# A macaron block on one core: the mixer's projections put ahead of its latents, and attention steps put among the last latents

## The chip, the cores and the metric

The kernel runs on one core of a Trainium2 chip. The metric is the device time of one execution in microseconds (us). The core has five engines that take instructions in their own order and wait for each other on semaphores: PE (matrix multiplication, TensorE), DVE (VectorE), ACT (ScalarE), POOL (GpSimd) and SP, which here only issues transfers.

## The reference

One layer on a sequence of 1024 rows of width 1024, in float32:

```
x = x + 0.5 * swiglu(rmsnorm(x), w1_gate, w1_up, w1_down)     # FFN 1, hidden 2816
h = rmsnorm(x) @ w_in    # columns: u 512 | v 512 | c_q 256 | c_kv 128 | k_rope 32
y_a = gelu(u) * (w_s (masked 128x128, per group) @ rmsnorm(gelu(v)) + b)
q  = rmsnorm(c_q)  @ w_uq      # 8 heads of 96 (64 plain + 32 rotary)
kv = rmsnorm(c_kv) @ w_ukv     # 8 heads of 64 (k) + 64 (v); k gets k_rope behind it
q, k = head rmsnorm, then rotation of the last 32 columns
y_b = softmax(q k^T * 96**-0.5, causal in chunks of 64) @ v
x = x + concat(rmsnorm(y_a), rmsnorm(y_b)) @ w_out
x = x + 0.5 * swiglu(rmsnorm(x), w2_gate, w2_up, w2_down)     # FFN 2
x = rmsnorm(x)
```

## The kernel before

Every float32 matrix product is done as three matmuls on operands split into a high and a low part (h and l in the names): hi*hi, hi*lo and lo*hi. Both FFNs use seven products where a plain 2x2 blocking needs eight (P1 to P7, `product`, matmuls at L464); the operands A11, A12, A21, S1 to S4 are quarters of a weight tile and sums of them, xB.. and xT.. the same of the input.

The code is issued step by step. A `Step` is one unit of work, in the order in which the steps are made; `st.before(lead, fn, floor)` puts a preparation (a load, a split) that many steps ahead of it, but not before step `floor`. `run_steps` then issues everything, and a scheduler arranges the instructions of each engine. Tiles of on-chip memory are handed out in a ring, so an instruction that writes a new tile may wait for the last reader of whatever stood there.

The mixer works on eight row tiles of 128 rows. Its steps are named by a letter and a number, and their order is a string in the code:

- u (L844 to L852): 24 matmuls of 512 columns for one row tile, gelu on ACT.
- m and g, for a pair of tiles: m (L859 to L861) is 12 matmuls of 256 columns; g multiplies by gelu(u) on DVE (L868), takes row norms (ACT square L286, POOL power L271) and stores the result to DRAM by two DMAs on POOL's queue (L875).
- a (`latent_in`): 24 matmuls of 416 columns (L722 to L724) for c_q, c_kv and k_rope; ACT copies them out (L770), takes squares (L773) and a square root (L277).
- c (`latent_T`): three transposes on PE (L881), then the split into `chl` by ACT (L290) and DVE (L291).
- k (`key_rope`): rotation of the shared key for two tiles, on POOL.
- l (`latent_tile`): 12 matmuls of 384 columns (L895 to L897) and 6 of 512 (L902 to L904) on `chl`; ACT copies qn (L919), kn (L918), squares (L921, L925) and takes the root r_qk (L277); DVE scales (L933, L934); POOL rotates q and k (L936, then L794, L796, L798).

The attention is a list of items (head, pair of row tiles); the n-th attention step does scores of item n, the transposes of the probabilities of item n-2 and its product with v, and the folding of item n-3. `head_T` (L982 transposes, L986 on ACT) makes the operands of a head. Probabilities are ACT's exp (L1003). Gelu, square root and exp each need another function table on ACT, seen as an instruction ACT_TABLE_LOAD under the line of the function that needs it.

The second FFN's steps are made by `gu2.steps(...)` (L1145): the first two weight tiles' raw quarters are loaded at the steps named by `load_at`, and the transposes of its normalized input (L300) run beside its first products. The first wait of its kind is for x tiles, stored by the first FFN in `x1d`.

Of the kernel before, what the change touches and what calls it, by code (L numbers as in the profile page):

```python
# [20 lines left out]
P = 128  # L21
# [3 lines left out]
NT = S // P  # L25
FH = 2816
NF = FH // P
GW = 512
H = 8
DN, DR, DV = 64, 32, 64  # L30
DQ = DN + DR
QL, KL = 256, 128
LAT = QL + KL + DR
# [27 lines left out]
def f(ap):  # L61
    return ap.bitcast(F32)
# [172 lines left out]
def block(nc, x, positions, ffn1_norm, ffn1_w_gate, ffn1_w_up,  # L235
# [4 lines left out]
    x = x[0]  # L240
    out = out[0]

    def tile_(shape, name, dt=F32):
        return nc.take("sb", shape, name, dt)
# [74 lines left out]
    steps = []  # L319
# [91 lines left out]
    LEAD_LOAD, LEAD_SUM, LEAD_SPLIT = 9, 3, 2  # L411

    class GateUp:
# [80 lines left out]
            t = self.h[u, d] = tile_([P, 512], f"h{d}_{self.tag}{u}")  # L494
            nc.vector.tensor_tensor(t, self.h[u, x0], self.h[u, x1], op=op)

        def steps(self, order, floor=0, loaded=(), load_at=()):
            at = {}
            for u, (pn, ka, kb, pair) in order:
                st = at[u, pn] = Step(lambda u=u, a=(pn, ka, kb, pair): self.product(u, *a))  # L500
                if pn == "P1":
                    for k in range(2):
                        if (u, k) not in loaded:
                            lead = st.index - load_at[u] if u < len(load_at) else LEAD_LOAD - k
                            st.before(lead, lambda u=u, k=k: self.load(u, k))
                if pn == "P6":
                    for which in range(2):
                        st.before(LEAD_SUM - which, lambda u=u, w=which: self.sums(u, w), floor)
                st.before(LEAD_SPLIT, lambda u=u, ka=ka: self.split(u, ka), floor)
            return at  # L510

    EARLY = [(0, BY_NAME["P1"]), (0, BY_NAME["P2"]), (1, BY_NAME["P1"]), (1, BY_NAME["P2"])]
    GU_ORDER = EARLY + [(u, p) for u in range(NU) for p in PRODUCTS if (u, p) not in EARLY]
# [136 lines left out]
    g1 = row_tile(ffn1_norm[0].partition_broadcast(P), "g1")  # L650
# [56 lines left out]
    mx = {"wv": [], "wa": [], "wu": [], "wuq": [], "v": [], "xm": {}, "u": {}, "q": {}, "k": {}, "vv": {}}  # L707
    wiv = w_in[0].rearrange("(k p) c -> p k c", p=P)

    def load_in(key, j, c0, width):  # L710
        mx[key, "raw", j] = load(tile_([P, 4, width], f"raw_{key}{j}"), wiv[:, 4 * j:4 * j + 4, c0:c0 + width])

    def split_in(key, k, width):
        raw = mx[key, "raw", k // 2]
        mx[key].append(q_split(raw[:, 2 * (k % 2):2 * (k % 2) + 2, :], [P, 2, width], f"{key}{k}"))
# [13 lines left out]
    def mix_norm_tile(t):  # L729
        xt = mx.pop(("x", t))  # L730
        xn = tile_([P, D], f"xnm{t}")
        normed(xt, mx["gm"], xn, f"m{t}")
        hv = transposed(xn, f"m{t}")
        xmh = tile_([P, KD, P], f"xmh{t}", F32R)
        xml = tile_([P, KD, P], f"xml{t}", F32R)
        for k in range(2):
            split(hv[k], xmh[:, 4 * k:4 * k + 4, :], xml[:, 4 * k:4 * k + 4, :])
        mx["xm"][t] = (xmh, xml)
# [4 lines left out]
    def v_tile(t):  # L743
        ps = bank(f"vps{t}")
        project(ps, mx["xm"][t], mx["wv"])
        vg = tile_([P, GW], f"vg{t}")
        nc.scalar.activation(vg, ps, AF.Gelu_apprx_tanh)
        sq = tile_([P, GW], f"vsq{t}")
        nc.gpsimd.tensor_tensor(sq, vg, vg, op=ALU.mult)
        ss = small(f"vss{t}", 4)  # L750
        nc.vector.tensor_reduce(ss, sq.rearrange("p (g c) -> p g c", g=4), axis=AX.X, op=ALU.add)
        r = rsqrt_mean(ss, f"v{t}", 4, 128)
        nc.vector.tensor_tensor(sq, vg, mx["gv"], op=ALU.mult)
        v3 = sq.rearrange("p (g c) -> p g c", g=4)
        nc.vector.tensor_tensor(v3, v3, r.unsqueeze(2).to_broadcast([P, 4, P]), op=ALU.mult)
        if t % 2 == 0:
            mx["v"].append([tile_([P, 2, GW], f"v{n}{t}", F32R) for n in "hl"])
        split(sq, mx["v"][-1][0][:, t % 2, :], mx["v"][-1][1][:, t % 2, :])
# [105 lines left out]
    def gmlp_pair(p):  # L864
        u, ps = mx["u"][p], mx.pop(("mix", p))
        for g in range(4):
            gs = slice(g * P, (g + 1) * P)
            nc.vector.scalar_tensor_tensor(u[:, :, gs], ps[:, g], bT[:, g:g + 1], u[:, :, gs],  # L868
                                           op0=ALU.add, op1=ALU.mult)
        for j in range(2):  # L870
            t = 2 * p + j
            ya = tile_([P, GW], f"ya{t}")
            r = row_rstd(u[:, j, :], ya, f"ya{t}", GW)
            nc.vector.scalar_tensor_tensor(ya, u[:, j, :], r, mx["goA"], op0=ALU.mult, op1=ALU.mult)
            nc.gpsimd.dma_start(yAd[rows(t), :], ya)  # L875
# [64 lines left out]
             mx["snq"][:, t:t + 1, :].to_broadcast([P, H, DR]), tab[:, 0], tab[:, 1])  # L940
        mx["q"][t], mx["k"][t], mx["vv"][t] = q_all, k_all, v_t

    vs = [Step(lambda t=t: v_tile(t)) for t in range(NT)]
    sm = {}
    works = {"u": u_tile, "m": mix_pair, "g": gmlp_pair, "a": latent_in, "k": key_rope, "c": latent_T, "l": latent_tile}
    for ch in ("u0 u1 m0 g0 u2 u3 m1 g1 a0 c0 a1 k0 l0 u4 c1 a2 l1 c2 a3 k1 l2 u5 m2 c3 a4 l3 g2 c4 a5 k2 l4 u6 "
               "c5 a6 c6 l5 a7 c7 k3 l6 u7 m3 l7").split():
        sm[ch] = Step(lambda f=works[ch[0]], n=int(ch[1]): f(n))
    v0 = vs[0].index
    vs[0].before(12, mix_gain)  # L950
    for t in range(4):
        steps[v0 - 5 + t].do(lambda t=t: mix_norm_tile(t))
    for t in range(4, NT):
        vs[t].before(4, lambda t=t: mix_norm_tile(t), v0)
    for j in range(2):
        vs[0].before(8 - j, lambda j=j: load_in("wv", j, GW, GW))
        sm["u0"].before(7 - j, lambda j=j: load_in("wu", j, 0, GW))
        sm["a0"].before(9 - j, lambda j=j: load_in("wa", j, 2 * GW, LAT))
    for k, (lv, lu, la) in enumerate(((4, 5, 7), (3, 5, 6), (2, 4, 5), (1, 3, 4))):
        vs[0].before(lv, lambda k=k: split_in("wv", k, GW))  # L960
        sm["u0"].before(lu, lambda k=k: split_in("wu", k, GW))
        sm["a0"].before(la, lambda k=k: split_in("wa", k, LAT))
    vs[0].before(3, v_gain)
    sm["u0"].before(3, spatial_weights)
    sm["u1"].before(0, out_gain)
    sm["a0"].before(6, load_uq)
    sm["a0"].before(4, latent_setup)
    sm["a0"].before(4, load_kv)
    sm["a0"].before(1, split_uq)
    sm["a0"].before(1, split_kv)  # L970
    sm["a0"].before(0, rope_tables)
    sm["l7"].do(lambda: mx.__setitem__("yB", [tile_([P, 4, H, DV], f"yB{i}") for i in range(2)]))

    def head_T(h, half):
        if half == 0:
            mx["qk", h] = [tile_([P, S], f"{n}{h}", F32R) for n in ("qh", "ql", "kh", "kl")]
        tiles = mx["qk", h]
        ps = big(f"T{h}_{half}")
        cs = slice(half * 512, (half + 1) * 512)
        for i, (src, col) in enumerate(((mx["q"], gqcol), (mx["k"], gkcol))):  # L980
            for t in range(4):
                nc.tensor.transpose(ps[:, i * 512 + t * P:i * 512 + (t + 1) * P], src[4 * half + t][:, h, :], ident)  # L982
        for i, col in enumerate((gqcol, gkcol)):
            hi, lo = tiles[2 * i], tiles[2 * i + 1]
            pv = ps[:, i * 512:(i + 1) * 512]
            nc.scalar.activation(hi[:, cs], pv, AF.Copy, scale=col)  # L986
            nc.vector.scalar_tensor_tensor(lo[:, cs], pv, col, f(hi[:, cs]), op0=ALU.mult, op1=ALU.subtract)
# [66 lines left out]
    D1, D2 = 2,3  # L1054
    ORDER = "PSTWF"
    TP = 2,3
    att = {}
    for n in range(len(items) + D2):
        st = att[n] = Step()
        if n == 0:  # L1060
            st.do(lambda: head_T(0, 0))
            st.do(lambda: head_T(1, 0))
        if n == 3:
            st.do(lambda: head_T(0, 1))
            st.do(lambda: head_T(1, 1))
        for op in ORDER:
            if op == "F" and D2 <= n:
                st.do(lambda i=items[n - D2]: folded(*i))
            if op == "P" and D1 <= n < len(items) + D1:
                st.do(lambda i=items[n - D1]: transposed_p(*i))  # L1070
            if n < len(items):
                h, pi = items[n]
                if op == "S":
                    st.do(lambda h=h, pi=pi: score_pair(h, pi))
                if op == "T" and 0 < h < H - 1 and pi in TP:
                    st.do(lambda h=h, pi=pi: head_T(h + 1, pi - TP[0]))
            if op == "W" and D1 <= n < len(items) + D1:
                st.do(lambda i=items[n - D1]: weighted(*i))

    att[0].do(lambda: gmlp_pair(3))  # L1080

    wov = w_out[0].rearrange("(k p) e -> p k e", p=P)
    wo = {}
# [58 lines left out]

    base2 = len(steps)
    gu2 = GateUp("b", xo2, ffn2_w_gate[0], ffn2_w_up[0], hds[1])
    gu2.steps(GU_ORDER, base2, load_at=(base2 - 1, base2))  # L1145
    rest(xo2, base2)

    def normalized(t, x3):
# [59 lines left out]
```

## Time and profile before

| what | value |
| --- | --- |
| time, median of 3 runs | 1774.74 us (1774.66 to 1776.48) |
| profiled execution, its own time | 1775.43 us |
| its span in the trace | 1773.4 us |
| mean granted TensorE clock | 0.989 of full speed |
| PE busy | 1714.4 us, 97% of the span |
| DVE, ACT, POOL busy | 1123.7, 757.0 and 149.5 us |

The span runs from the first to the last instruction on the core; the 2.0 us around it are start and end. The granted clock is given as a share of 2.4 GHz, 0.5 being the other level, 1.2 GHz. A wait in the trace is put down to the engine that came last.

### The profile page before, as it was taken

What the parts mean: (1) busy time and instruction counts of PE and PEld (TensorE: products, weight loads), DVE (VectorE), ACT (ScalarE), POOL (GpSimd) and SP (SyncE); (2) the same over time, 40 slices, a digit from 0 to 9 for tenths busy, and PEclk for the clock granted to TensorE, in tenths of its full rate; (3) what the DMA queues carried; (4) which work ended last, traced back from release to release, by engine and by line L of the source; (5) the groups of instructions that cost most, each with busy time, mean ns of one, the idle gap of its engine ahead of it and who ended that gap; (6) DMA issues with size and microseconds to landing.
All of it is one profiled execution on the core that took longest, in us unless ns stands there. A gap on an engine that the chain in (4) does not pass through costs nothing.

```text
span 1773.4 us, 21088 instructions
## 1 busy us (share of the span) xinstructions
PE 1714.4 (97%) x8132; PEld 1439.8 (81%) x8132; DVE 1123.7 (63%) x1497; ACT 757.0 (43%) x1151; POOL 149.5 (8%) x287
## 2 busy tenths in 40 slices
PE   7999999999999999988799999999999999999998
PEld 5788888888888888877699888778888888888886
DVE  7966556545578666554877644684656655558774
ACT  7523333334334444444777833352333233433442
POOL 2000000000000013322300511100000000000010
PEclk9999999999999999998899999999999999999999
DMA  6323232226844521200000332424233222683531
GB/s 202 115 93 119 98 111 89 96 89 220 311 129 162 183 85 48 69 10 3 13 1 1 120 101 87 140 95 137 76 120 108 95 90 90 231 301 110 179 129 48
DMA packets 122979, 199.48 MB, mean 112 GB/s; under 512 B 11008, under 2 KB 57600, under 8 KB 122880
## 3 DMA queue, kind: packets, MB, share of 16 engines
q1 hardware_dynamic: 118784, 184.52, 30.7%
q0 software_dynamic: 3520, 12.58, 1.8%
q8 instruction: 63, 1.03, 0.2%
q10 hardware_dynamic: 576, 1.05, 0.2%
q14 instruction: 36, 0.29, 0.0%
HBM read 143.07 MB, written 55.05 MB: 112 GB/s over the span
## 4 chain that ended last, share of the span: by engine, by line
PE 89%; DVE 4%; ACT 3%; DMA 1%; POOL 1%; issue 1%; SPq 0%; POOLq 0%; ACTq 0%; DVEq 0%
PE psum L464 45%; PE psum L594 8%; PE psum L596 8%; PE psum L597 8%; PE psum L1026 2%; PE psum L722 2%; PE psum L724 2%; PE psum L723 2%; PE psum L1125 1%; PE psum L1126 1%; PE psum L1128 1%; PE psum L300 1%; PE psum L1036 1%; PE psum L1035 1%; PE psum L997 1%
## 5 line engine op out<-in xcount | busy, mean ns | idle before, releaser
L480 DVE TENSOR_TENSOR P_b<-psum,P_b 128x1024 f32<-128x1024 f32 x33 | 40.3, 1222 | 93.0 <-PE psum L464 93.0
L480 DVE TENSOR_TENSOR P_a<-psum,P_a 128x1024 f32<-128x1024 f32 x33 | 40.3, 1222 | 91.8 <-PE psum L464 91.8
L470 ACT COPY P_b<-psum 128x1024 f32<-128x1024 f32 x33 | 33.4, 1014 | 70.3 <-PE psum L464 68.3
L470 ACT COPY P_a<-psum 128x1024 f32<-128x1024 f32 x33 | 33.4, 1013 | 69.1 <-PE psum L464 69.1
L271 POOL TENSOR_TENSOR r_fin<-ms_fin,mhalf 128x1 f32<-128x1 f32 x8 | 8.0, 1009 | 609.4 <-DVE ms_fin L269 609.3
L291 DVE TENSOR_TENSOR pl<-psum,ph 128x512 fp32r<-128x512 f32 (+1 forms) x80 | 48.5, 630 | 10.8 <-ACT ph L290 10.2
L481 ACT ACTIVATE P_a<-P_a 128x512 f32<-128x512 f32 x33 | 20.8, 631 | 80.8 <-DVE P_a L480 80.7
L1001 DVE TENSOR_REDUCE nm<-psum 128x1 f32<-128x128 f32 (+3 forms) x64 | 46.8, 749 | 11.8 <-PE psum L999 11.5
L481 ACT ACTIVATE P_b<-P_b 128x512 f32<-128x512 f32 x33 | 20.8, 632 | 73.0 <-DVE P_b L480 72.9
L1125 PE MATMUL psum<-woh,yh 128*128 128x512 f32 x128 | 50.5, 396 | 0.0
L1003 ACT ACTIVATE p<-psum,nm 128x128 f32<-128x128 f32 (+3 forms) x64 | 47.7, 750 | 6.4 <-DVE nm L1001 3.4
L1126 PE MATMUL psum<-wol,yh 128*128 128x512 f32 x128 | 50.2, 392 | 0.0
L703 POOL DMA_DIRECT2D x1d<-x_a x8 | 4.6, 580 | 510.6 <-DVE x_a L608 510.5
L1026 PE MATMUL psum<-ident,p 128*128 128x128 f32 x288 | 43.4, 281 | 3.8 <-ACT p L1003 3.8
L1128 PE MATMUL psum<-woh,yl 128*128 128x512 f32 x128 | 44.9, 391 | 0.0
L290 ACT CAST ph<-psum 128x512 fp32r<-128x512 f32 (+1 forms) x80 | 41.7, 559 | 7.0 <-PE psum L1026 6.8
L1036 PE MATMUL psum<-pl,vv 128*128 128x256 f32 x160 | 42.7, 293 | 1.2 <-DVE pl L291 1.2
L1035 PE MATMUL psum<-ph,vv 128*128 128x256 f32 x160 | 43.3, 294 | 0.2 <-ACT ph L290 0.2
L997 PE MATMUL psum<-kh,qh 128*128 128x512 f32 (+2 forms) x96 | 38.6, 404 | 1.0 <-ACT kh L986 0.9
L1026 PEld LDWEIGHTS psum<-ident,p 128*128 128x128 f32 x288 | 34.0, 145 | 6.4 <-ACT p L1003 4.8
L608 DVE SCALAR_TENSOR_TENSOR x_b<-psum,x_b 128x512 f32<-128x512 f32 x32 | 21.0, 686 | 26.9 <-PE psum L597 26.9
L464 PE MATMUL psum<-xB11h_f,A11h_a 128*128 128x512 f32 x88 | 35.4, 405 | 2.6 <-ACT xB11h_f L389 2.6
(525 smaller groups left out, 5753.3 us busy)
## 6 DMA issues: line engine op xcount, KB each, us to landing
raw_a<-in_ffn_w_gate SPq DMA_DIRECT2D x22, 512.0 KB, 4.3
raw_a<-in_ffn_w_up SPq DMA_DIRECT2D x22, 512.0 KB, 5.4
hd<-hS_a SPq DMA_DIRECT2D x44, 256.0 KB, 2.2
raw_b<-in_ffn_w_gate SPq DMA_DIRECT2D x22, 512.0 KB, 4.2
raw_b<-in_ffn_w_up SPq DMA_DIRECT2D x22, 512.0 KB, 5.2
hd<-hS_b SPq DMA_DIRECT2D x44, 256.0 KB, 2.1
aS_a<-hd SPq DMA_DIRECT2D x20, 512.0 KB, 4.2
wB_a<-in_ffn_w_down SPq DMA_DIRECT2D x20, 512.0 KB, 5.6
```

The lines of the kernel that those rows point to most:

```text
L464: mm(o, lhs[:, 4 * m + k, :], rhs[:, k, :], start=pn in FIRST and n == 0, stop=n == 11, skip_group_check=True)
L470: nc.scalar.copy(ev[u, pn], bk)
L480: nc.vector.tensor_tensor(c, bk, c, op=ALU.add)
L594: mm(banks[t], hh[:, j, tl], dh[:, j, :], start=pn in DOWN_FIRST and c == 0 and j == 0, stop=False, skip_group_check=True)
L596: mm(banks[t], hh[:, j, tl], dl[:, j, :], start=False, stop=False, skip_group_check=True)
L597: mm(banks[t], hl[:, j, tl], dh[:, j, :], start=False, stop=c == 5, skip_group_check=True)
L1026: nc.tensor.transpose(ps[:, i * P:(i + 1) * P], prs[j][:, c * P:(c + 1) * P], ident)
L1035: mm(acc[:, 0:256], mx["vv"][c][:, h, :], hi, start=i == 0, stop=False)
L1036: mm(acc[:, 0:256], mx["vv"][c][:, h, :], lo, start=False, stop=i == len(pts) - 1)
L1125: mm(pe[e], yh[:, k, :], wh[:, es], start=k == 0, stop=False)
L1126: mm(pe[e], yh[:, k, :], wl[:, es], start=False, stop=False)
L1128: mm(pe[e], yl[:, k, :], wh[:, e * 512:(e + 1) * 512], start=False, stop=k == KD - 1)
```

## The change

The work stays the same; its order changes in two places.

In the mixer the string of steps puts all u, m and g steps ahead of the first a. The first three attention steps (x0 to x2), which were behind the last latent tile, stand among the last ones; for this their functions move up in the file as they are, with the loop's body as `attend(n)`. The buffer yB is made in the step n == 2.

In the second FFN everything starts one step earlier: the floor of its splits becomes `base2 - 1`, each raw quarter of the first two weight tiles gets its own step for its load, and the split for the third product made is one step ahead of it and not two.

```
-    for ch in ("u0 u1 m0 g0 u2 u3 m1 g1 a0 c0 a1 k0 l0 u4 c1 a2 l1 c2 a3 k1 l2 u5 m2 c3 a4 l3 g2 c4 a5 k2 l4 u6 "
-               "c5 a6 c6 l5 a7 c7 k3 l6 u7 m3 l7").split():
+    for ch in ("u0 u1 m0 g0 u2 u3 m1 g1 u4 u5 m2 g2 u6 u7 m3 g3 a0 c0 a1 k0 l0 c1 a2 l1 c2 a3 k1 l2 c3 a4 l3 c4 a5 k2 l4 "
+               "c5 a6 c6 a7 l5 c7 k3 x0 l6 x1 l7 x2").split():
+        if ch[0] == "x":
+            attend(int(ch[1]))
+            continue
         sm[ch] = Step(lambda f=works[ch[0]], n=int(ch[1]): f(n))
...
-    sm["l7"].do(lambda: mx.__setitem__("yB", [tile_([P, 4, H, DV], f"yB{i}") for i in range(2)]))
...
-    att[0].do(lambda: gmlp_pair(3))
+    for n in range(3, len(items) + D2):
+        attend(n)
...
-                            lead = st.index - load_at[u] if u < len(load_at) else LEAD_LOAD - k
+                            lead = st.index - load_at[u, k] if (u, k) in load_at else LEAD_LOAD - k
...
-                st.before(LEAD_SPLIT, lambda u=u, ka=ka: self.split(u, ka), floor)
+                st.before(LEAD_SPLIT if len(at) != 2 else 1, lambda u=u, ka=ka: self.split(u, ka), floor)
...
-    gu2.steps(GU_ORDER, base2, load_at=(base2 - 1, base2))
+    gu2.steps(GU_ORDER, base2 - 1, load_at={(0, 0): base2 - 2, (0, 1): base2 - 1, (1, 0): base2, (1, 1): base2})
```

What stands on the engines. First ACT, around the second latent tile (qn1, kn1, vv1, sq.. are its copies and squares, r_qk its root, chl2 the split for the third). Before:

```order
L919 COPY qn1_6689<-psum_70 128x8x96 [waits PE_49]
L294 ACTIVATE vv1_6697<-psum_70,rl_6301 128x8x64 [waits DVE_49,PE_49]
L925 ACTIVATE sq1_0_6706<-qn1_6689 128x384 [waits Activation_49]
L918 COPY kn1_6692<-psum_70 128x8x64 [waits DVE_49]
L921 ACTIVATE sk1_6703<-kn1_6692 128x512 [waits Activation_49]
L925 ACTIVATE sq1_1_6711<-qn1_6689 128x384 [waits DVE_49]
L852 ACT_TABLE_LOAD
L852 ACTIVATE u2_6596<-psum_70 128x512 [waits PE_49]
L277 ACT_TABLE_LOAD
L277 ACTIVATE r_qk1_6716<-ssq1_6698 128x16 [waits DVE_49]
L290 CAST chl2_6741<-psum_70 128x384 [waits Activation_49,Pool_49]
```

After:

```order
L919 COPY qn1_6850<-psum_70 128x8x96 [waits PE_49]
L925 ACTIVATE sq1_0_6870<-qn1_6850 128x384 [waits Activation_49]
L925 ACTIVATE sq1_1_6873<-qn1_6850 128x384
L294 ACTIVATE vv1_6858<-psum_70,rl_6483 128x8x64 [waits PE_49]
L290 CAST chl2_6902<-psum_70 128x384 [waits DMASW6_49,PE_49]
L770 COPY at0_6471<-psum_70 128x416 [waits PE_49]
L773 ACTIVATE jk3_6931,ssl_6480<-at0_6471 128x256 [waits Activation_49]
L918 COPY kn1_6853<-psum_70 128x8x64 [waits DVE_49]
L773 ACTIVATE jk3_6931,ssl_6480<-at0_6471 128x128
L773 ACTIVATE jk3_6931,ssl_6480<-at0_6471 128x32
L921 ACTIVATE sk1_6865<-kn1_6853 128x512 [waits Activation_49]
L277 ACTIVATE rl_6483<-ms_c3_6935 128x2 [waits DVE_49]
```

The gelu of u2 with its two table loads has left this place, and chl2 waits for PE's transposes and an older DMA, no longer for POOL.

Second, ACT among the last latents (p.. are exps of the first attention items, qh and kh operands of the heads, L972 after is L1003 before, L955 is L986). Before:

```order
L986 ACTIVATE qh1_7555<-psum_70,gqcol_95 128x512 [waits PE_49]
L277 ACTIVATE r_qk6_7410<-ssq6_7393 128x16 [waits DVE_49]
L918 COPY kn7_7488<-psum_70 128x8x64 [waits DVE_49]
L921 ACTIVATE sk7_7500<-kn7_7488 128x512 [waits Activation_49]
L986 ACTIVATE qh0_7534<-psum_70,gqcol_95 128x512 [waits PE_49]
L986 ACTIVATE kh0_7538<-psum_70,gkcol_96 128x512 [waits PE_49]
L986 ACTIVATE kh1_7559<-psum_70,gkcol_96 128x512 [waits DVE_49]
L277 ACTIVATE r_qk7_7511<-ssq7_7494 128x16 [waits DVE_49]
L286 ACTIVATE ya6_7598,ss_ya6_7599<-u3_7160 128x512
L1003 ACT_TABLE_LOAD
L1003 ACTIVATE p0_0_7581,rs0_0_7574<-psum_70,nm0_0_7578 128x128 [waits DVE_49]
L1003 ACTIVATE p0_1_7590,rs0_0_7574<-psum_70,nm0_1_7586 128x256 [waits DVE_49]
```

After:

```order
L972 ACT_TABLE_LOAD
L972 ACTIVATE p0_0_7491,rs0_0_7484<-psum_70,nm0_0_7488 128x128 [waits DVE_49]
L972 ACTIVATE p0_1_7499,rs0_0_7484<-psum_70,nm0_1_7496 128x256 [waits DVE_49]
L294 ACTIVATE vv6_7529<-psum_70,rl_6483 128x8x64 [waits PE_49]
L972 ACTIVATE p0_2_7578,rs0_1_7570<-psum_70,nm0_2_7574 128x384 [waits DVE_49]
L972 ACTIVATE p0_3_7586,rs0_1_7570<-psum_70,nm0_3_7583 128x512 [waits DVE_49]
L277 ACT_TABLE_LOAD
L277 ACTIVATE r_qk5_7407<-ssq5_7389 128x16 [waits DVE_49]
L972 ACT_TABLE_LOAD
L972 ACTIVATE p1_0_7679,rs1_0_7672<-psum_70,nm1_0_7676 128x128 [waits DVE_49]
L918 COPY kn6_7524<-psum_70 128x8x64 [waits DVE_49]
L919 COPY qn7_7608<-psum_70 128x8x96 [waits DMASW5_49,PE_49]
```

The exps of the first items stand ahead of the roots of the tiles 5 to 7, each change of function with a table load: three between the last chl and the first later score before, seven after. In the whole stretch from the first a it is ten before and eight after.

Third, SP at the second FFN's start (raw.. are the weight quarters, x2 reads x1d back). Before:

```order
L311 DMA x2_7_10899<-x1d_86 128x1024 [waits DVE_49,PE_49]
L311 DMA x2_5_10730<-x1d_86 128x1024 [waits DMAHW6_49,DVE_49,PE_49]
L311 DMA x2_6_10810<-x1d_86 128x1024 [waits DMAHW4_49,DMAHW7_49,DVE_49,PE_49]
L311 DMA raw1_b0_10894<-in_ffn2_w_gate 128x4x256 [waits DMAHW0_49,DMASW5_49,DMAHW2_49,DMASW4_49,DMAHW6_49,DVE_49,Activation_49]
L311 DMA raw1_b0_10894<-in_ffn2_w_up 128x4x256 [waits DMAHW1_49]
L311 DMA raw1_b1_10997<-in_ffn2_w_gate 128x4x256 [waits PE_49]
L311 DMA raw1_b1_10997<-in_ffn2_w_up 128x4x256 [waits DMAHW3_49]
L311 DMA raw0_b1_10992<-in_ffn2_w_gate 128x4x256 [waits PE_49]
L311 DMA raw0_b1_10992<-in_ffn2_w_up 128x4x256 [waits DMAHW5_49]
L311 DMA raw0_b0_10890<-in_ffn2_w_gate 128x4x256 [waits DVE_49]
L311 DMA raw0_b0_10890<-in_ffn2_w_up 128x4x256 [waits DMAHW7_49]
```

After:

```order
L311 DMA x2_6_10844<-x1d_86 128x1024 [waits DMAHW2_49,DMASW4_49,DMAHW5_49,DVE_49,Activation_49]
L311 DMA raw0_b0_10840<-in_ffn2_w_gate 128x4x256 [waits DMAHW6_49,DVE_49,Activation_49]
L311 DMA raw0_b0_10840<-in_ffn2_w_up 128x4x256 [waits DMAHW7_49]
L311 DMA x2_5_10760<-x1d_86 128x1024 [waits DMAHW0_49,PE_49]
L311 DMA raw1_b0_10924<-in_ffn2_w_gate 128x4x256 [waits DMASW5_49,DMAHW0_49,DVE_49,DMAHW1_49,PE_49,Activation_49]
L311 DMA raw1_b0_10924<-in_ffn2_w_up 128x4x256
L311 DMA raw1_b1_11029<-in_ffn2_w_gate 128x4x256 [waits DMAHW3_49,PE_49]
L311 DMA raw0_b1_11024<-in_ffn2_w_gate 128x4x256 [waits DMASW6_49,DMAHW4_49,DVE_49,DMAHW5_49,PE_49,Activation_49]
L311 DMA raw0_b1_11024<-in_ffn2_w_up 128x4x256
L311 DMA raw1_b1_11029<-in_ffn2_w_up 128x4x256 [waits DMAHW6_49]
L311 DMA x2_7_10935<-x1d_86 128x1024 [waits DMAHW7_49,PE_49]
```

The load of raw0_b0 stands ahead of x2_5, and that of x2_7 behind the other quarters.

## Rows read from the trace of the kernel before

**Rows 1.** Page, part 1: busy time of each engine
```profile
PE 1714.4 (97%) x8132; PEld 1439.8 (81%) x8132; DVE 1123.7 (63%) x1497; ACT 757.0 (43%) x1151; POOL 149.5 (8%) x287
```

**Rows 2.** Windows around the mixer's u and latent stage
```profile
core 0: us, PE busy (x) PEld busy (x) DVE busy (x) ACT busy (x) POOL busy (x), PEclk, DMA share, GB/s
700.00:732.70 32.70, 32.70 (x156) 27.50 (x155) 19.30 (x31) 12.51 (x21) 9.98 (x11) 1.00 0.24 75
732.70:875.10 142.40, 117.09 (x558) 102.91 (x556) 81.44 (x226) 75.29 (x179) 49.14 (x102) 0.90 0.04 12
732.70:837.50 104.80, 90.79 (x428) 81.44 (x427) 51.27 (x151) 49.21 (x120) 33.72 (x68) 0.92 0.03 11
763.68:830.82 67.14, 55.75 (x252) 49.26 (x252) 34.52 (x98) 29.81 (x69) 20.57 (x40) 0.90 0.02 9
765.00:770.00 5.00, 5.00 (x16) 4.61 (x16) 0.50 (x4) 0.00 (x0) 0.00 (x0) 0.50 0.00 0
837.50:875.10 37.60, 26.30 (x132) 21.48 (x130) 30.18 (x75) 26.07 (x60) 15.42 (x34) 0.86 0.04 15
```

**Rows 3.** Timeline of PE: steps from start to start (start, length, line)
```profile
818.49 0.35 PE L722 MATMUL psum<-wa_h,xmh 128*128 128x416 f32 x1
818.68 0.35 PE L723 MATMUL psum<-wa_l,xmh 128*128 128x416 f32 x1
...
836.51 0.49 PE L881 MATMUL psum<-ident,at 128*128 128x128 f32 x3
...
840.62 0.39 PE L722 MATMUL psum<-wu_h,xmh 128*128 128x512 f32 x1
840.85 0.39 PE L723 MATMUL psum<-wu_l,xmh 128*128 128x512 f32 x1
```

**Rows 4.** Timeline of ACT: chl casts, a table load
```profile
763.68 0.48 ACT L290 CAST chl<-psum 128x384 fp32r<-128x384 f32 x1 [0.94 <-POOL qn L798]
...
776.84 1.28 ACT L277 ACT_TABLE_LOAD   x1
778.13 0.22 ACT L277 ACTIVATE r_qk<-ssq 128x16 f32<-128x16 f32 x1
783.86 0.48 ACT L290 CAST chl<-psum 128x384 fp32r<-128x384 f32 x1 [5.51 <-POOL qn L798]
...
830.82 0.48 ACT L290 CAST chl<-psum 128x384 fp32r<-128x384 f32 x1 [5.47 <-POOL qn L798]
```

**Rows 5.** Timeline of POOL, one tile's rope
```profile
781.12 1.06 POOL L794 TENSOR_TENSOR rt<-qn,late 128x256 f32<-128x256 f32 x1 [1.16 <-DVE qn L933]
...
783.09 0.73 POOL L798 TENSOR_TENSOR qn<-rt 128x256 f32<-128x256 f32 x1
```

**Rows 6.** Waits, 745 to 880 us (total, times, longest)
```profile
ACT qn L919 <- PE psum L897: 25.1, 5, 6.0
...
ACT chl L290 <- POOL qn L798: 14.7, 4, 5.5
```

**Rows 7.** Second FFN's start: PE waits, 1100 to 1180 us
```profile
PE psum L464 <- DVE S2l_b L450: 2.2, 1, 2.2
PE psum L464 <- DVE xT1l_f L390: 2.1, 1, 2.1
PE psum L464 <- ACT b_f L364: 1.3, 1, 1.3
```

**Rows 8.** Second FFN's start: timeline of PE, then DVE
```profile
1145.93 1.03 PE L300 MATMUL psum<-ident,xn_f 128*128 128x128 f32 x8
...
1148.14 0.69 DVE L379 TENSOR_TENSOR t_f<-b_f,b_f 128x512 f32<-128x512 f32 x1
...
1155.61 1.22 DVE L450 TENSOR_TENSOR S2l_b<-S_b,S2h_b 128x1024 fp32r<-128x1024 f32 x1
...
1163.02 2.35 DVE L390 TENSOR_TENSOR xT1l_f<-b_f,xT1h_f 128x1024 fp32r<-128x1024 f32 x2
```

More of the change, by code (lines that the diff above doesn't have):

```diff
@@ L495, in hsum, with steps @@
             nc.vector.tensor_tensor(t, self.h[u, x0], self.h[u, x1], op=op)
-        def steps(self, order, floor=0, loaded=(), load_at=()):
+        def steps(self, order, floor=0, loaded=(), load_at={}):
             at = {}
@@ L941, in latent_tile @@
         mx["q"][t], mx["k"][t], mx["vv"][t] = q_all, k_all, v_t
-    vs = [Step(lambda t=t: v_tile(t)) for t in range(NT)]
-    sm = {}
-    works = {"u": u_tile, "m": mix_pair, "g": gmlp_pair, "a": latent_in, "k": key_rope, "c": latent_T, "l": latent_tile}
-    for ch in ("u0 u1 m0 g0 u2 u3 m1 g1 a0 c0 a1 k0 l0 u4 c1 a2 l1 c2 a3 k1 l2 u5 m2 c3 a4 l3 g2 c4 a5 k2 l4 u6 "
-               "c5 a6 c6 l5 a7 c7 k3 l6 u7 m3 l7").split():
[L948 to L971, printed above, removed]
-    sm["l7"].do(lambda: mx.__setitem__("yB", [tile_([P, 4, H, DV], f"yB{i}") for i in range(2)]))
     def head_T(h, half):
@@ L1057, in block, with attend @@
     att = {}
-    for n in range(len(items) + D2):
+    def attend(n):
         st = att[n] = Step()
@@ L1062, in block @@
             st.do(lambda: head_T(1, 0))
+        if n == D2 - 1:
+            st.do(lambda: mx.__setitem__("yB", [tile_([P, 4, H, DV], f"yB{i}") for i in range(2)]))
         if n == 3:
@@ L1078, in block @@
                 st.do(lambda i=items[n - D1]: weighted(*i))
-    att[0].do(lambda: gmlp_pair(3))
+    vs = [Step(lambda t=t: v_tile(t)) for t in range(NT)]
+    sm = {}
+    works = {"u": u_tile, "m": mix_pair, "g": gmlp_pair, "a": latent_in, "k": key_rope, "c": latent_T, "l": latent_tile}
+    for ch in ("u0 u1 m0 g0 u2 u3 m1 g1 u4 u5 m2 g2 u6 u7 m3 g3 a0 c0 a1 k0 l0 c1 a2 l1 c2 a3 k1 l2 c3 a4 l3 c4 a5 k2 l4 "
[3 more added lines that the diff above has]
+            continue
+        sm[ch] = Step(lambda f=works[ch[0]], n=int(ch[1]): f(n))
+    v0 = vs[0].index
+    vs[0].before(12, mix_gain)
+    for t in range(4):
+        steps[v0 - 5 + t].do(lambda t=t: mix_norm_tile(t))
+    for t in range(4, NT):
+        vs[t].before(4, lambda t=t: mix_norm_tile(t), v0)
+    for j in range(2):
+        vs[0].before(8 - j, lambda j=j: load_in("wv", j, GW, GW))
+        sm["u0"].before(7 - j, lambda j=j: load_in("wu", j, 0, GW))
+        sm["a0"].before(9 - j, lambda j=j: load_in("wa", j, 2 * GW, LAT))
+    for k, (lv, lu, la) in enumerate(((4, 5, 7), (3, 5, 6), (2, 4, 5), (1, 3, 4))):
+        vs[0].before(lv, lambda k=k: split_in("wv", k, GW))
+        sm["u0"].before(lu, lambda k=k: split_in("wu", k, GW))
+        sm["a0"].before(la, lambda k=k: split_in("wa", k, LAT))
+    vs[0].before(3, v_gain)
+    sm["u0"].before(3, spatial_weights)
+    sm["u1"].before(0, out_gain)
+    sm["a0"].before(6, load_uq)
+    sm["a0"].before(4, latent_setup)
+    sm["a0"].before(4, load_kv)
+    sm["a0"].before(1, split_uq)
+    sm["a0"].before(1, split_kv)
+    sm["a0"].before(0, rope_tables)
+    for n in range(3, len(items) + D2):
+        attend(n)
     wov = w_out[0].rearrange("(k p) e -> p k e", p=P)
```

## The prediction

> **What bounds the kernel now.** The page's busy times come first: PE works 1714.4 us, 97% of the span, so nearly all of the kernel is matmul time, and a change of order can win only where PE stands still or runs at the lower clock [rows 1]. The windows say where that is. In the u stage, 700 to 732.7, PE is busy for every one of 32.7 us at clock 1.00, and DVE, ACT and POOL have room (19.3, 12.5 and 10.0 us). In the latent stage behind it, 732.7 to 875.1, PE is busy for 117.1 of 142.4 us at a mean clock of 0.90; in the five microseconds from 765 it is busy throughout, but at 0.50 [rows 2].
>
> Why it stands still there is read from ACT's timeline and the waits. The cast of chl, which PE's latent matmuls need, starts at 783.86 and at 830.82 behind 5.5 us of waiting for POOL's rotation of an earlier tile's q [rows 4, 6]. That rotation ran from 781.12 to 783.82 and the cast began 0.04 us later [rows 5]. chl does not compute with q, so this is a place in memory that comes free. ACT then waits 25.1 us in five times for the q matmuls [rows 6]. So the latent tiles go round a loop: PE, ACT, DVE, POOL, PE. From 763.68 to 830.82, four tiles take 67.14 us, 16.8 a tile, with PE at work for 55.75 of them [rows 2, 4].
>
> **The change part by part.** All prices are for the profiled execution of 1775.43 us (span 1773.4), which is 0.7 above the median of 1774.74. I compare one stretch: from the first matmul of a0 to the first score of a later item, 142.4 us before. I cut it where the last chl is cast, into 104.8 and 37.6 [rows 2].
>
> *Moved ahead.* Four u and two m steps leave this stretch for the u stage. A u matmul starts 0.23 us after the one before it (840.62, 840.85), so 24 take 5.5 us and four steps 22.0 [rows 3]. An m matmul has half the columns, 0.115 us, so 12 take 1.4 and two steps 2.8. PE was never idle in the u stage, so these 24.8 us are paid in full, at full clock. Their gelus, squares and DVE products go along: per pair a few us of ACT and DVE, which are 38% and 59% busy there [rows 2]. I price these at nothing; without that cover the last pair's g, four DVE products and two norms, would end behind a0's matmuls, where it still delays only buffers. The stores of y_a on POOL's queue and the later load of the kv weights on SP have tens of microseconds until they are read: nothing.
>
> *The latents without fillers, up to the last chl.* PE needs for a tile: a, 24 x 0.19 = 4.56 us; c, 0.50; l, 12 matmuls of three quarters of u's width, 12 x 0.17 = 2.1, and 6 of u's width, 6 x 0.23 = 1.4 [rows 3]. Eight a and c and six l come before the last chl: 8 x 5.06 + 6 x 3.5 = 61.4 us. That is one bound: PE never waits. The other: 104.8 less the fillers that stood in it, three u and one and a half m, 16.5 + 2.1 = 18.6, gives 86.2, if all of PE's idle and slow time stays. If the fillers stood in waits that stay, not even those 18.6 come off and it remains 104.8. Which is nearer? The new order has no chl that waits for POOL, and the next a stands ahead of the l whose results are awaited. DVE was busy 34.5 us in four tiles [rows 2], 8.6 a tile with a g step among them that now leaves, and PE needs 8.56: nearly balanced, so small waits remain and the clock will dip with them. I let the stage keep the mean clock of 0.90 and price that as ten per cent: 61.4 / 0.90 = 68.2 us. Six of this part's seven table loads go as well, 6 x 1.28 = 7.7 us of ACT [rows 4], already in that value.
>
> *The tail, from the last chl to the later score.* Before 37.6 us, with DVE busy 30.2 and ACT 26.1 [rows 2]. The last u and g leave it, but exps now alternate with square roots: seven table loads for three, 4 x 1.28 = 5.1 us more on ACT. ACT alone makes a lower bound of 26.1 + 5.1 = 31.2; the upper is 37.6 + 5.1 = 42.7, nothing hidden and nothing gained. I take the middle, 37.
>
> In rows, a load takes 1.28 us and the next activation starts 0.01 us behind its end (776.84 + 1.28, then 778.13) [rows 4]. The Trainium skill, "ScalarE: Activation LUTs", section "What ACT_TABLE_LOAD costs", puts a switch at 1283 ns and some 1380 ns of draining, 2.66 us in all, and its "Rules for kernel authors" would finish one set of functions before the next; by this the alternation would make an estimated 9.6 us more in the tail (7 x 2.66 - 7 x 1.28), and most of the gain would go. The 1283 ns agree with the row; a drain behind the load does not show there.
>
> Sum of the mixer: 24.8 + 68.2 + 37 = 130.0 against 142.4, so -12.4.
>
> *The second FFN's start.* PE waits 2.2 + 2.1 + 1.3 = 5.6 us there [rows 7]. In the new order one product of 24 matmuls, 5.5 us, stands between the last transposes and the first matmul that needs xT1; on DVE four instructions of 0.69, two of 1.22 and a pair of 2.35 stand ahead of xT1l, 7.6 us, and its first half takes 1.2 [rows 8]. With ACT's copy out of the transposes the result is there some 9.6 us after they end: a wait of 4.1, in place of the three. I take -1.5. The bounds: -5.6 if all waits go; and if DVE keeps its place (xT1l from 1163.02, first half done 18.4 us after the transposes began at 1145.93), a wait of 18.4 - 5.5 = 12.9, which is 7.3 more than now. The last x2 load stands behind four quarters on SP; it is the mishap that would bring that upper bound.
>
> Total: -12.4 - 1.5 = -13.9, so 1775.43 - 13.9 = 1761.5 for a run like the profiled one; less the 0.7 to the median, 1761.
>
> **The rivals.**
>
> *PE becomes the only bound.* For: no chl waits for POOL, DVE without the g steps needs less than PE a tile. Both parts at their lower bounds: 24.8 + 61.4 + 31.2 = 117.4, that is -25.0, with the FFN -26.5, so 1748. Against: two heavy chains would have to dovetail without a gap.
>
> *The tail eats it.* For: ACT is the engine with most new work there, exp and root in turn, and scores wait for exps. The tail at 42.7 instead of 37: 5.7 less gain, 1767. With the page's drain on top it would be 1771.
>
> *No change.* For: the wait of ACT for the q matmuls (25.1 us) is larger than the one for POOL (14.7) [rows 6], so the POOL gate may be a symptom. If three quarters of the 24.8 us by which 86.2 exceeds 61.4 stay, part one takes 80.0, the stretch 141.8, and with the FFN the time is 1772 to 1773.
>
> *Slower.* The mechanism: the u and m steps were the only work that PE could do while a tile's chain ran through ACT and DVE; with nothing beside the chain PE stands idle once per tile and falls to the lower clock, as at 765. Place: a0 to the last chl. It decides from 142.4 - 24.8 - 37 = 80.6 us for that part, 10.1 a tile. With all of the present loss kept, 86.2, the stretch takes 148.0: +5.6, with the FFN +4.1, so 1779; with half the fillers' cover missing too, 95.5, +13.4, so 1788. For it: the 0.50 in the row at 765. Against: those slow stretches follow the waits for POOL, and a of the next tiles (4.56 us each) remains as a filler.
>
> The Trainium skill, "TensorE: Matmul & The Clock Gate", section "HAM oscillation", describes just this: matmul groups parted by waits that start each time at the lower clock. The row at 765 agrees that it happens in this stage; no row shows it for the new order.
>
> **How the numbers follow.** Chances: the forecast 0.56, PE-bound 0.08, tail 0.14, no change 0.11, slower 0.11. A measurement of this kernel tells 0.2%, 3.5 us, from no change. So faster is 0.56 + 0.08 + 0.14 = 0.78, same 0.11, slower 0.11. The forecast's own range is 1754 to 1768. The range of 8 in 10 goes from 1749, the end of the PE-bound case, to 1775, past the no-change case; slower cases are mostly left out.
>
> **What would show it.** In the new trace: the u stage some 24.8 us longer with PE full at 1.00; a0 to the last chl near 68 us and no wait of chl for POOL; the tail near 37 with seven table loads; at the second FFN's start one wait of some 4 us for xT1l. I am wrong if the first part is above 80 us with PE at 0.50 in much of it, if the tail is above 43, or if the transposes of xn7 wait for the late x2 load by more than 7 us.

## The result and the profile after

The changed kernel takes 1756.24 us (median; 1754.53 to 1758.07) against 1775.08 for the kernel before on the same chip: a ratio of 0.9893, interval 0.9876 to 0.9910, or 18.8 us less. Forecast were 1761 and a range of 1749 to 1775. The profiled execution has a span of 1755.0 us, 18.4 less than before.

The page of the changed kernel, busy times and the granted clock by slices:

```profile
PE 1707.4 (97%) x8132; PEld 1434.0 (82%) x8132; DVE 1122.8 (64%) x1497; ACT 753.0 (43%) x1149; POOL 151.5 (9%) x287
...
PEclk9999999999999999999899999999999999999999
```

PE's busy time fell by 7 us with the same 8132 matmuls [rows 1]: that part of the gain is time at the lower clock. Cut at the same instructions, the two traces give this account of the span, in us ((0,2) is the attention item of head 0 and the third pair of row tiles):

```
from / to                                   before    after   change
start to first u matmul                     708.19   708.75    +0.56
first u to first matmul of a0                24.65    49.33   +24.68
first matmul of a0 to last chl cast         104.68    61.35   -43.33
last chl cast to first score of (0,2)        37.55    34.72    -2.83
to first matmul of the output projection    154.14   155.17    +1.03
to first A22 matmul of the second FFN       151.32   151.29    -0.03
to the end                                  592.87   594.39    +1.52
```

The windows of the changed kernel (us, then busy time of PE, PEld, DVE, ACT and POOL, granted clock, DMA share, GB/s): the u stage, the latents, the tail, two pieces of the tail, and a piece of the second FFN's start.

```profile
708.75:758.08 49.33, 49.33 (x242) 41.78 (x240) 21.71 (x40) 16.83 (x30) 15.83 (x28) 1.00 0.23 78
758.08:819.43 61.35, 61.35 (x339) 58.87 (x338) 42.74 (x147) 37.69 (x115) 25.57 (x54) 1.00 0.03 10
819.43:854.15 34.72, 20.37 (x100) 15.80 (x98) 28.65 (x65) 27.18 (x54) 14.36 (x28) 0.79 0.00 0
839.43:844.43 5.00, 0.66 (x4) 0.42 (x4) 4.13 (x12) 4.72 (x8) 1.01 (x3) 0.87 0.01 2
844.43:849.43 5.00, 1.34 (x4) 0.57 (x4) 4.86 (x13) 1.50 (x3) 3.29 (x6) 0.50 0.00 0
...
1135.00:1140.00 5.00, 4.37 (x12) 3.46 (x13) 5.00 (x5) 4.08 (x5) 0.00 (x0) 0.67 0.00 0
```

The u stage took the moved steps at full clock, as its window before had promised [rows 2]. The latents are the surprise: PE is busy for the whole 61.35 us at clock 1.00, where the windows before showed 0.90 to 0.92 and gaps [rows 2]. The tail is still poor: PE works 0.66 us in one piece of 5 us, and the 1.34 us that it works in the next run at 0.50.

ACT's timeline, casts of chl, and the waits that answer to [rows 4, 6]:

```profile
767.50 0.48 ACT L290 CAST chl<-psum 128x384 fp32r<-128x384 f32 x1 [1.60 <-PE psum L881]
...
776.01 0.47 ACT L290 CAST chl<-psum 128x384 fp32r<-128x384 f32 x1
...
784.96 0.47 ACT L290 CAST chl<-psum 128x384 fp32r<-128x384 f32 x1
...
819.43 0.50 ACT L290 CAST chl<-psum 128x384 fp32r<-128x384 f32 x1
```

```profile
ACT qn L919 <- PE psum L897: 8.6, 5, 4.1
...
ACT chl L290 <- PE psum L881: 2.6, 2, 1.6
```

No cast waits for POOL any more. ACT waits 8.6 us for q matmuls instead of 25.1, though nothing in ACT's or PE's work on a latent tile was changed.

PE's waits in the tail, from 819 to 855:

```profile
PE psum L951 <- DVE kn L934: 7.9, 2, 5.7
PE psum L951 <- POOL qn L798: 2.9, 2, 1.5
PE psum L995 <- ACT p L972: 2.5, 1, 2.5
...
```

PE's waits from 1080 to the end, and its timeline at the second FFN's start (answering to [rows 7, 8]; L594 is in the last down projection):

```profile
PE psum L594 <- ACT aS4h_b L567: 1.7, 1, 1.7
PE psum L464 <- DVE xT1l_f L390: 1.5, 1, 1.5
PE psum L464 <- ACT xT1h_f L389: 1.3, 1, 1.3
...
```

```profile
1133.36 0.73 PE L464 MATMUL psum<-xT1h_f,S1h_b 128*128 128x512 f32 x2 [1.25 <-ACT xT1h_f L389]
1135.63 0.50 PE L464 MATMUL psum<-xT1l_f,S1h_b 128*128 128x512 f32 x1 [1.54 <-DVE xT1l_f L390]
...
1137.06 0.63 PE L464 MATMUL psum<-xT1h_f,S1h_b 128*128 128x512 f32 x1
1137.48 0.63 PE L464 MATMUL psum<-xT1l_f,S1h_b 128*128 128x512 f32 x1
```

The three waits of 5.6 us became two of 2.8. But PE then ran for some microseconds with 0.42 us from matmul to matmul (1137.06, 1137.48) in place of 0.23, the lower clock that the window from 1135 shows as 0.67, and the whole start took the same 151.3 us. A second execution of this kernel, below, has the same two waits without the lower clock.

### The profile page after: what moved, and what is told of

It is laid out like the page before. It is cut to its first block, busy times and chain, and to the rows that moved or that the text cites. A ratio compares the mean times of both kernels' runs of the same rounds, so it can differ in the third digit from the quotient of the medians.

```text
span 1755.0 us, 21054 instructions
## 1 busy us (share of the span) xinstructions
PE 1707.4 (97%) x8132; PEld 1434.0 (82%) x8132; DVE 1122.8 (64%) x1497; ACT 753.0 (43%) x1149; POOL 151.5 (9%) x287
## 4 chain that ended last, share of the span: by engine, by line
PE 90%; DVE 4%; DMA 2%; ACT 2%; SPq 1%; issue 1%; POOL 1%; POOLq 0%; ACTq 0%; DVEq 0%
PE psum L464 44%; PE psum L594 8%; PE psum L597 8%; PE psum L596 8%; PE psum L724 2%; PE psum L722 2%; PE psum L723 2%; PE psum L995 2%; PE psum L1131 2%; PE psum L1132 2%; PE psum L1134 2%; PE psum L300 1%; PE psum L1005 1%; PE psum L1004 1%; PE psum L966 1%; PE psum L967 1%
## 5 line engine op out<-in xcount | busy, mean ns | idle before, releaser
L972 ACT ACTIVATE p<-psum,nm 128x128 f32<-128x128 f32 (+4 forms) x64 | 47.8, 752 | 3.1 <-DVE nm L970 2.0
```

## The experiments

Ratios are to the kernel before on the same chip. "Latents" is first matmul of a0 to last chl cast, "tail and attention" from there to the last score, "FFN start" first matmul of the output projection to first A22 matmul, all read from the timelines; before: 104.68, 180.35 and 151.32 us; changed: 61.35, 177.25 and 151.29. Each is read from one trace: two traces of the changed kernel differ by 1.0 us in tail and attention and by 1.3 in the FFN start, and two of the old latents by 3.8 us, so stage differences of that size say little. The theory at first: the u and m steps between the latent tiles were the harm, and moving them the gain. The rival, from the cast at 783.86: chl waited for a buffer that POOL's rotation had just read, and the order hardly matters. The first four split the change into its parts.

**Mixer part alone.**

```
-    gu2.steps(GU_ORDER, base2 - 1, load_at={(0, 0): base2 - 2, ...})
+    gu2.steps(GU_ORDER, base2, load_at=(base2 - 1, base2))      # and steps() as before
```

> The change without its second-FFN part. Theory A (read from the two traces: from the first output-projection matmul to the first A22 matmul of the second FFN 151.3 us in both): the FFN part brings nothing, so this is within 1.5 us of the changed kernel, 1755 to 1758. Theory B (the prediction's term of -1.5, with waits of 5.6 us before): 1757.7 or more, and the waits on S2l and b_f are back in its trace.

Measured 0.9864 (0.9845 to 0.9883), 1749.2 us. Neither number came: its median is lower than that of the whole change. Latents 61.36, FFN start 145.08. PE's only wait in that start:

```profile
PE psum L464 <- DVE xT1l_f L390: 0.9, 1, 0.9
```

In this order the last transposes stand 40 matmuls ahead of the first product that needs a sum, and S2 comes before S1; in the changed kernel they stand 24 ahead, and S1 comes first. So the waits of the kernel before went without any edit of the second FFN: the scheduler's order there had moved with the mixer's.

**Second-FFN part alone.**

```
-    gu2.steps(GU_ORDER, base2, load_at=(base2 - 1, base2))
+    gu2.steps(GU_ORDER, base2 - 1, load_at={(0, 0): base2 - 2, ...})   # on the kernel before
```

> The second-FFN part alone on the kernel before. Theory A: no gain, 1774 to 1776; one wait of some 3 us for xT1 instead of three, and about as much lost again to a stretch at the lower clock behind it. Theory B: -1.5, 1773.6, with the clock at 1.00 throughout the second FFN's start.

Measured 0.9971 (0.9961 to 0.9982), 5.1 us less. Theory A fell, and B's size was too small: FFN start 145.99, at a clock of 1.00. Beside the old mixer the part has a gain; beside the new one, the run above leaves none. Not all of the difference between the two traces is the part's: the latents, whose order on PE, ACT, DVE and POOL is that of the kernel before, took 100.89 us here against 104.68, with the same gaps on PE (14.1 and 14.0 us) and more of the matmuls at full clock. The latents of the kernel before, then of this one, and its five microseconds from 765:

```profile
732.84:837.52 104.68, 90.67 (x427) 81.32 (x426) 51.12 (x151) 49.23 (x121) 33.72 (x68) 0.92 0.03 11
732.74:833.63 100.89, 86.76 (x427) 77.61 (x426) 51.49 (x151) 49.22 (x120) 33.71 (x68) 0.97 0.04 12
765.00:770.00 5.00, 5.00 (x26) 4.32 (x25) 1.58 (x5) 2.17 (x4) 0.00 (x0) 1.00 0.00 0
```

**Fillers ahead, attention steps behind l7.**

```
-   "... c5 a6 c6 a7 l5 c7 k3 x0 l6 x1 l7 x2"
+   "... c5 a6 c6 l5 a7 c7 k3 l6 l7 x0 x1 x2"
```

> All u, m and g ahead of the latents, but the latents' own order as before (l5 ahead of a7) and the first three attention steps behind l7. Both theories: a0 to the last chl at PE's own speed, 61 to 64 us. Theory A (moving the fillers ahead is the gain; the attention steps among the last latents are worth little since ACT and its seven table loads bound that tail): 1755 to 1760. Theory B (the attention steps are what PE needs to stay at work in the tail): the tail of 34.7 us grows by the 6 to 8 us of matmul work that now stands behind l7, 1762 to 1765.

The edit also puts l5 back ahead of a7. Measured 0.9880 (0.9864 to 0.9897). Latents and the first 35 us behind them:

```profile
757.48:819.41 61.93, 61.93 (x338) 59.52 (x337) 45.25 (x149) 39.87 (x118) 28.85 (x60) 1.00 0.04 14
819.41:854.41 35.00, 24.72 (x128) 21.00 (x127) 29.49 (x68) 23.16 (x49) 13.41 (x24) 0.80 0.00 1
```

As Theory A had it, the attention steps among the last latents bring nothing: tail and attention take 172.61 us, 4.6 less than with them, and from the last chl on ACT has three table loads where the change has seven. The FFN start takes 144.28 us, the shortest of all, with the second-FFN part in. The total shows less of it, because the last stretch took 601.32 us in place of 594.39, with PE waiting 4.5 us for weight splits in the last down projection.

**Fillers as before, attention steps among the latents.**

```
-   "... m2 g2 u6 u7 m3 g3 a0 c0 a1 k0 l0 c1 ..."      # attention as in the change
+   "... a0 c0 a1 k0 l0 u4 c1 a2 l1 c2 a3 k1 l2 u5 m2 c3 a4 l3 g2 c4 a5 k2 l4 u6 c5 a6 c6 a7 u7 l5 c7 k3 m3 x0 g3 l6 x1 l7 x2"
```

> The u, m and g steps among the latents as before (the last ones, u7, m3 and g3, a little earlier, since buffers leave no room otherwise), the attention steps among the last latents as in the change, and the change's second-FFN part. Theory A (the gain is from the fillers' move): casts of chl still wait for POOL, a0 to the last chl some 100 us, the time 1770 to 1777. Theory B (the attention steps among the latents bring it): 1760 to 1766.

Measured 0.9991 (0.9981 to 1.0002). Theory A: latents 104.70, and the wait is there:

```profile
ACT chl L290 <- POOL qn L798: 12.0, 3, 5.5
```

So far the move of the fillers looks like the cause. The next four ask why, with the changed kernel again beside them.

**The changed kernel again.**

> The changed kernel as it is, on the chip on which the next three run, for a direct comparison with the run without its second-FFN part (0.9864 of before). Theory A (together with the new mixer the second-FFN part costs some 5 us): 0.989 to 0.990 of before, out-projection to first A22 matmul 151 us. Theory B (the chips differ, the part does nothing): 0.986 to 0.987 and about 145 us.

Measured 0.9893 (0.9878 to 0.9908); FFN start 150.00. The intervals of this and the mixer part alone overlap, so the totals don't settle which is faster; the FFN start (150 to 151 against 145.1) goes with Theory A. Its wait for the second half of xT1 and the window behind it:

```profile
1133.81 0.50 PE L464 MATMUL psum<-xT1l_f,S1h_b 128*128 128x512 f32 x1 [1.54 <-DVE xT1l_f L390]
1135.00:1140.00 5.00, 5.00 (x23) 4.13 (x23) 5.00 (x5) 3.94 (x5) 0.00 (x0) 1.00 0.08 12
```

The order is the same and so are the two waits, 1.25 and 1.54 us, but the lower clock did not follow them here.

**One buffer kept for the rotation, everything else as before.**

```
-        tab = tile_([P, 2, H, DR], f"rt{t}")
+        if t == 0:
+            mx["rt"] = tile_([P, 2, H, DR], "rt")
+        tab = mx["rt"]
```

> The kernel before, with one buffer rt for the rotation of all tiles in place of a new one for each: POOL writes and reads it in its own order, so nothing waits more, and chl no longer lands on a buffer that POOL has just read (no cast of chl waits for POOL in the order). Theory A (that wait is what paced the latents before): a0 to the last chl falls from 104.7 to 85-95 us, the time by 10 to 20. Theory B (it is a symptom, the u and m matmuls in PE's queue between a tile's a, c and l are what hurts): another wait takes its place, a0 to the last chl stays at 100 to 105, and the time moves by under 4 us.

Measured 0.9875 (0.9862 to 0.9889), 1750.6 us, no less a gain than the whole change, and more than Theory A's 10 to 20 us. Its latents (all fillers still in them), two casts of chl and its waits:

```profile
733.37:812.67 79.30, 79.30 (x420) 73.87 (x419) 50.13 (x150) 49.15 (x121) 31.60 (x67) 1.00 0.05 15
```

```profile
757.46 0.48 ACT L290 CAST chl<-psum 128x384 fp32r<-128x384 f32 x1 [0.67 <-DVE ssq L926]
...
769.75 0.48 ACT L290 CAST chl<-psum 128x384 fp32r<-128x384 f32 x1 [0.62 <-DVE ssq L926]
```

```profile
ACT qn L919 <- PE psum L897: 12.4, 5, 4.9
...
ACT chl L290 <- DVE ssq L926: 2.0, 3, 0.7
```

79.30 us with PE busy throughout at 1.00, where Theory A had 85 to 95 (420 matmuls stand in that stretch, 427 in it before); 104.68 - 79.30 = 25.4 us gone, or 21.6 against the 100.89 of the second-FFN part alone. Keeping rt moves the later tiles in the ring, and chl now waits for DVE's reading of a square, 0.7 us at most. From the first u matmul to the last score it takes 286.07 us, the changed kernel 287.93, the kernel before 309.68. My first theory fell here: with the buffer kept, the fillers between the latent tiles harm nothing.

**No gelu loads among the latents.**

```
-    ... ps, AF.Gelu_apprx_tanh)
+    ... ps, AF.Gelu_apprx_tanh if t < 4 else AF.Copy)
```

> The kernel before, with the gelu of the row tiles 4 to 7 of u left out (a plain copy stands in its place), so that ACT does not go to the gelu table and back among the latents. Theory A (the alternation gelu/root holds up roots and casts): a0 to the last chl falls by about the six loads, 6 x 1.28 = 7.7 us, or more. Theory B (the loads fall into ACT's waits for PE and POOL, 25.1 and 14.7 us before): under 2 us.

Measured 0.9972 (0.9960 to 0.9983). Latents and the wait:

```profile
732.67:829.93 97.26, 86.91 (x427) 77.73 (x426) 51.49 (x151) 41.40 (x115) 33.86 (x68) 0.95 0.04 12
```

```profile
ACT chl L290 <- POOL qn L798: 13.3, 3, 6.3
```

The whole fell by 5.0 us, more than Theory B's 2. The latents fell by 7.4 us against the trace of before, near Theory A's 7.7 for six loads at 1.28 us, but by 3.6 against the 100.89 that the same order took in the second-FFN part alone; PE's gaps went from 14.0 to 10.4 us. So the direction is Theory A's, and the size is open between 3.6 and 7.4. By the Trainium skill, "ScalarE: Activation LUTs", section "What ACT_TABLE_LOAD costs", six switches at some 2.66 us would be an estimated 16.0; the run does not show that much. I take it that ACT's loads lie on the loop that POOL's wait paces, since a root that comes late makes the rotation late; the run does not show that step by itself.

**Fillers ahead, attention behind, second FFN as before** (the edits of the first and third).

> All u, m and g ahead, attention steps behind l7, and the second FFN as before. Theory A (each part's effect on its own place holds: a0 to the last chl 61-62, from there to the last score 172.6, second FFN's start 145 as without that part, the end at 592): 1741 to 1745. Theory B (a later place gives it back, as the end of that mixer with the second-FFN part did by 9 us): 1749 to 1755.

Measured 0.9854 (0.9841 to 0.9868), 1747.7 us: between the theories. Latents 61.94 and the end 592.44 as hoped, but tail and attention 174.72 and FFN start 147.34. Against the run of the same mixer with the second-FFN part, the FFN start is 3.1 us longer and the last stretch 8.9 shorter.

**The change with the kept buffer** (the edit of the kept buffer on the changed kernel).

> The changed kernel with one buffer rt kept for the rotation of all tiles. Theory A (the change's mixer part and the kept buffer take away the same loss): no more than 2 us from the changed kernel (0.9893 of before), 1753 to 1756; a0 to the last chl stays at 61.35, since PE has no idle time there. Theory B (two separate gains): 10 us or more below it.

Measured 0.9916 (0.9902 to 0.9929), 1760.8 us. Latents 61.55: the buffer gives nothing a second time, as Theory A has it. But the total missed it, to the worse: tail and attention 180.14 and the end 598.49, where the last down projection waits 3.0 us for aS4h.

**The kept buffer with the second-FFN part, old mixer** (both edits on the kernel before).

> The kernel before with the kept buffer rt and the second-FFN part of the change, the mixer's order as before. Theory A (the second-FFN part is worth its 5 us where its products stand in the order that they have with the old mixer: transposes of the last x tile ahead of 37 matmuls, S2 before S1): 5 us below the run with the kept buffer alone, 1745 to 1747, first output product to A22 at 144 to 146 us. Theory B (chance of the order, no stable gain): 1749 to 1752.

Measured 0.9839 (0.9826 to 0.9853), 1746.4 us; FFN start 145.99, as with that part alone on the kernel before, and 149.29 with the kept buffer alone. Theory A.

**Fillers ahead, attention behind, second FFN as before, with the kept buffer** (the edit of the kept buffer on that kernel).

> All u, m and g ahead, attention steps behind l7, second FFN as before, and the kept buffer. Theory A (no loss left that the buffer could take away): within 2 us of the same kernel without the kept buffer (0.9854), 1746 to 1749. Theory B: 1740 or less, with the tail from the last chl below 28 us.

Measured 0.9852 (0.9838 to 0.9865), 1748.3 us, Theory A; tail and attention 173.95.

**As the run before, u7 and m3 left in the tail.**

```
-   "... m2 g2 u6 u7 m3 g3 a0 ... l5 a7 c7 k3 l6 l7 x0 x1 x2"
+   "... m2 g2 u6 a0 ... a7 l5 c7 k3 l6 u7 m3 l7 x0 g3 x1 x2"
```

> As the run before, but u7 and m3 stay among the last latents as work for PE while their chains run, and the last g among the first attention steps. Theory A (the tail is bound by ACT's and DVE's chain, with PE idle for 10 us or more, so matmuls put there are free): 5 to 6 us below the run before, 1740 to 1743. Theory B (the gelu, its two table loads and g's work on ACT and DVE lengthen that chain by as much): 1746 to 1750.

The edit also puts a7 ahead of l5, as in the change. Measured 0.9825 (0.9811 to 0.9838), 1743.8 us, the lowest median of all: 4.5 us below the run before, a little less gain than Theory A has. From the first u matmul to the last score only 2.8 us of it lie; 2.6 lie in the FFN start (146.04 against 148.60), which the edit leaves alone. First 35 us of its tail, and PE's waits there:

```profile
813.17:848.17 35.00, 27.05 (x147) 23.34 (x146) 30.36 (x72) 28.10 (x58) 18.63 (x37) 0.85 0.04 16
```

```profile
PE psum L953 <- POOL qn L798: 2.3, 2, 1.8
PE psum L953 <- DVE kn L934: 1.6, 1, 1.6
PE psum L953 <- ACT p L974: 1.4, 1, 1.4
...
```

PE works 27.05 us where it worked 20.4 of 34.7 in the changed kernel, by about the 6.9 us of u7 and m3, and the wait for kn is 1.6 us instead of 7.9. But the matmuls there are not free, as Theory A has it: against the run before, the stage ahead of a0 is 6.9 us shorter, and tail and attention are 4.0 us longer.

## Why the prediction was right, and where it was not

**The sum.** That the total came within 5 us is in part luck. The mixer up to the first score of (0,2) gained 21.5 us where 12.4 were forecast; 1.5 of the other 9.1 went in the second FFN and 3.1 in places that I had not priced.

**What bounds.** I read the cast of chl as waiting for "a place in memory that comes free". That was the cause: with one buffer kept, and no step moved, the latents lost 25.4 us, 21.6 by the other trace of the old order.

**Moved ahead.** 24.8 us priced, 24.68 measured.

**The latents.** This is the mis-sized term: 68.2 us taken, 61.35 measured, my lower bound of 61.4. The step that failed is "I let the stage keep the mean clock of 0.90": without PE's gaps the lower clock did not come, so its losses were not to be paid again. The ground for remaining waits was poor too: DVE was busy for 42.7 of 61.35 us, not "nearly balanced" with PE. My 8.6 us a tile was a wrong reading of the kernel before: these casts of chl stand between the two that I took as four tiles apart,

```profile
783.86 0.48 ACT L290 CAST chl<-psum 128x384 fp32r<-128x384 f32 x1 [5.51 <-POOL qn L798]
789.40 0.48 ACT L290 CAST chl<-psum 128x384 fp32r<-128x384 f32 x1
811.74 0.48 ACT L290 CAST chl<-psum 128x384 fp32r<-128x384 f32 x1 [2.80 <-POOL qn L798]
824.79 0.46 ACT L290 CAST chl<-psum 128x384 fp32r<-128x384 f32 x1
```

so from 763.68 to 830.82 it is five tiles, 13.4 us each and not 16.8, with 6.9 us of DVE.

Why the gain came was only half told: I gave it to the new order, and a kernel with the old order and the kept buffer gains as much. That the new order set its buffers so that no chl lands behind POOL is read from its waits; a new order with that wait put back was not run.

**The tail.** 37 taken, 34.72 measured, between the bounds. It is not a gain of the attention steps: moving them behind l7 (with l5 ahead of a7) makes tail and attention shorter, by 4.6 us with the change's second FFN and by 7.3 without (182.03 to 174.72).

**The second FFN.** -1.5 taken, -0.03 measured, -1.3 in the second execution. The wait for xT1 was there, 2.8 for the 4.1 forecast; in the first execution the lower clock behind it, which I had not priced, took back about what the second one gained. Alone, the part is worth 5 us. Over all runs the start goes with the scheduler's order: where 34 to 54 matmuls stand between the last transposes and the first product that needs a sum, it takes 144.3 to 148.6 us, and where 24 or 30 do, 149.2 to 151.6. The same edit gave 24 (the change), 37 (alone), 48 and 54, so the edit alone does not settle it; no run moved that number by itself. Not priced either: +1.0 in the attention, +1.5 in the last stretch, +0.6 ahead.

**The rivals.** PE as only bound came true for the latents alone. Slower and no change fell with the clock at 1.00. The tail as the place where it is eaten: by the runs 2.8 us (u7 and m3 left in it) to 7.3 us (attention steps behind l7) lie there, not the whole gain. Its 1771 is the 9.6 us on top of 1761, not on top of the 1767 beside it.

Open: why the kernels with both the moved fillers and the new second FFN (the changed one, its repeat, and the two more with both) wait 1.7 to 4.5 us in the last down projection and take 594 to 601 us for the last stretch, where the others take 592 to 593. The order of the instructions there was not taken apart.

## What to carry to other kernels

When an engine waits for another that does not feed it, look for the buffer that the one has just read; keep that buffer apart before moving any step. Price a stage that has lost its gaps at full clock, and leave the lower clock to the bound. Time parts alone and together: the second-FFN part was worth 5 us alone (0.9971), and beside the new mixer (0.9864 without it, 0.9893 with it) no gain of it shows. Before pricing a few microseconds of one stage, look at a second trace of the same order.

## What the runs showed of the hardware

A gap on PE can cost twice. In the kernel before, the latents held 14.0 us without a matmul (104.68 less 90.67 busy), yet lost 25.4 us to the kept buffer's version, the rest being matmuls at the lower clock, as in the piece at 0.50 [rows 2]. In the run of the second-FFN part alone the gaps were 14.1 us and that rest only 7.5.

So the lower clock does not follow a gap each time. PE's first matmul behind the wait for the second chl, in the kernel before and in that run, whose order on the engines is the same there:

```profile
764.21 0.69 PE L895 MATMUL psum<-wuq0h,chl 128*128 128x384 f32 x1 [1.92 <-ACT chl L290]
```

```profile
764.11 0.44 PE L895 MATMUL psum<-wuq0h,chl 128*128 128x384 f32 x1 [1.92 <-ACT chl L290]
```

Behind the same gap of 1.92 us the next five microseconds ran at 0.50 in one execution and at 1.00 in the other. The two waits of 1.25 and 1.54 us in the second FFN did the same: 0.67 behind them in one execution of the changed kernel, 1.00 in the other.
